# Decay and rate of an RWKV-7 layer: two small matmuls, once per block of 448 tokens instead of once per step of 128

## The chip, the cores and the metric

The kernel runs on one core of a Trainium2 chip. The metric is the device time of one execution in microseconds. Times given are from the hardware profiler and from repeated timed runs. The engines: TensorE (PE, with its weight loads PEld), VectorE (DVE), ScalarE (ACT), GpSimd (POOL) and SyncE (SP), which here issues almost all DMAs, in its program order.

## The reference

One inference step of one hybrid decoder layer, with 2048 prompt tokens and 64 sample tokens (8 requests of 8). The width is 1024. One input projection gives everything: `z = h @ w_in`. Its first 1792 columns are mixed with those of the token before (`zs = z + (z_prev - z) * mu`) and feed an RWKV-7 mixer of 8 heads of 64; the others feed a pooling mixer and two gates. Then follow an output projection and a feed-forward part of 4096. The lines that the change is about:

```python
r = zs[..., :512]; k = zs[..., 512:1024]; v = zs[..., 1024:1536]
lw = zs[..., 1536:1600]          # 64 columns
la = zs[..., 1600:1664]          # 64 columns
w_log = -softplus(-(decay0 + tanh(lw) @ w_decay2)) - 0.5      # w_decay2: 64 x 512
decay = exp(-exp(w_log))
a_in  = sigmoid(a0 + la @ w_a2)                                # w_a2: 64 x 512
kk = k * k_k, normalised per head; k = k * (1 + (a_in - 1) * k_a)
s  = s * decay + (s @ -kk) (kk * a_in)^T + v k^T ; y = s @ r   # per token, per head
```

## The kernel before

The 2112 tokens are cut into five blocks. A block is the width of most matmuls: 384, 448, 448, 448 (384 of the prompt and the 64 sample tokens, block 3) and 384 columns. Activations lie with the features on the 128 partitions and the tokens along the row. A large product is made of three fp32r matmuls, high × high, high × low and low × high, since each operand is split into two parts: a high part, rounded to fp32r by a ScalarE cast (L166), and a low part, the rest, from a VectorE subtraction (L167). A unit of weights is 512 KB, loaded by `load_unit` into `raw` (2 buffers) and split into `whi` and `wlo` (3 buffers each); 24 matmuls use a unit.

Stage A of a block (`stage_A`) is the input projection. Ten tiles of 128 columns come first, numbered m = 12, 13, 0 to 7 (`lerp_tile`): a tile has 24 matmuls into one PSUM tile (`pi`) of the ring `mm` of four. VectorE scales it into `zr` (L476), ScalarE and VectorE do the shift (`zs`, L495 and L496), and a DMA stores it to the DRAM tensor `zd` of the block (L506). m = 12 holds `lw` on its first 64 rows and `la` on the other 64. `zr`, `zs` and many more come from the ring `st`, five tiles of 128x512. Behind tile 7 `values` follows: tokens on the rows, four units `wv_0` to `wv_3`, each used for all token tiles in turn; three of its PSUM tiles (`pv`) come from the ring `mm`, and a fourth from the ring `wk` of three. Then come pooling tiles and gates (`gt`).

The recurrence is worked in 17 steps, k0 to k15 of 128 prompt tokens and k16 of the 64 sample tokens (`wkv_sub`). A step first loads what it wants from `zd`: `lw` and `la` (L1040), `zk` and `zr` (L1043), 256 KB each, and the two matrices with their constant rows (L1046, L1047). Then tanh on `lw` (L1050), four fp32 matmuls `psd` of K = 65 (64 rows and a row of ones for the constant), a ScalarE tanh with the factor 0.5 into `td` (L1055), and the same for `psa` and `ta` (L1060); a sigmoid is written as a tanh. VectorE adds one to `td` (L1062), scans and so on; much later in the step come the norm products `pnb` (from `cs` and from `zk`, L1091), the chunk matrices (`p`, `pt`, `pg`) and the state.

All of TensorE's instructions are chained in the order in which the program emits them (`TensorOrder.issue`). That order is woven from a main stream (stages by `ORDER = "A0 A1 A2 M0 A3 F0 M1 A4 F1 M2 F2 M3 F3 M4 F4"`) and the steps: each step is a generator, and a `yield` with a number says how many microseconds of TensorE time are to pass before the next piece. That time is counted by the planner from the costs in `matmul` (`T.now`), not measured. The lists of the other engines are in program order too, as a scheduler places them. In the trace every matmul has the line L150, whatever asks for it.

Of the kernel before, what the change touches and what calls it, by code (L numbers as in the profile page):

```python
# [67 lines left out]
def hybrid_step(ctx: ExitStack, tc: tile.TileContext, a: dict, outs: list):  # L68
# [149 lines left out]
    for b, (g0, n, s) in enumerate(blocks):  # L218
# [4 lines left out]
        yd.append(dr.tile([n + s, DA], F32, name=f"yd{b}"))  # L223
        xd.append(dr.tile([DM, n + s], F32, name=f"xd{b}"))
    wbd = dr.tile([DP, DM], F32, name="wbd")
    vsd = dr.tile([NS, LS + 1, DA], F32, name="vsd")

    def segs(g, n):
# [172 lines left out]
    consts.close()  # L401
    g2c = kp.tile([P, 8], F32, name="g2c")
    G.dma_start(out=g2c, in_=a["norm2_g"].rearrange("(k p) -> p k", p=P))
    consts.close()
    ready = set()
    done = {"p": 0, "s": False, "pooling": False}
# [78 lines left out]
    def lerp_tile(b, hs, m):  # L485
        g0, n, s = blocks[b]
        nt = n + s
        ci = smap[m]
        raw = st(f"zr{b}_{m}")
        zs = st(f"zs{b}_{m}")  # L490
        V.tensor_copy(raw[:, 0:1], carry[:, ci:ci + 1])

        def evac(sz, ps):
            scaled_out(b, raw[:, 1:1 + sz], ps)
            S.activation(zs[:, :sz], raw[:, 1:1 + sz], AF.Copy, scale=omu[:, m:m + 1])  # L495
            V.scalar_tensor_tensor(zs[:, :n], raw[:, 0:n], mu[:, m:m + 1], zs[:, :n], op0=ALU.mult, op1=ALU.add)  # L496
            V.tensor_copy(carry[:, ci:ci + 1], raw[:, n:n + 1])
            if s:
                zp = sp.tile([P, NS, LS], F32, tag="zp", name=f"zp{b}_{m}", bufs=1)
                rv = raw[:, 1 + n:1 + nt].rearrange("p (s t) -> p s t", t=LS)  # L500
                V.tensor_copy(zp[:, :, 1:], rv[:, :, :LS - 1])
                V.tensor_copy(zp[:, :, 0:1], sst[:, ci].unsqueeze(2))
                V.scalar_tensor_tensor(zs[:, n:nt], zp.rearrange("p s t -> p (s t)"), mu[:, m:m + 1], zs[:, n:nt],
                                       op0=ALU.mult, op1=ALU.add)
                V.tensor_copy(shs[:, ci].unsqueeze(2), rv[:, :, LS - 1:LS])
            D.dma_start(out=zd[b][ci * P:(ci + 1) * P, :], in_=zs[:, :nt])  # L506

        yield from col_tile(b, hs, m, evac)

    def values(b, hs):  # L510
        g0, n, s = blocks[b]
# [164 lines left out]
    def stage_A(b):  # L676
        hs = hs_of.pop(b)
        done["pooling"] = True
        if b:
            dgs[b] = diagonals(r1_of[b], tok_tiles(b), f"r1d{b}")  # L680
        for i, m in enumerate((12, 13, 0, 1, 2, 3, 4, 5, 6, 7)):
            if i > 2:
                tick()
            yield from lerp_tile(b, hs, m)
        yield from values(b, hs)
        ready.add(b)
        us = None
        for i, m in enumerate(range(18, 34)):
            done["pooling"] = i < 9
            tick()  # L690
            if i % 2 == 0 and i <= 8:
                if us is not None:
                    pool_state(i // 2 - 1, us)
                if i < 8:
                    us = yield from pool_tile(b, hs, i // 2)
                    tick()
            yield from gate_tile(b, hs, m)
        yield from flush()
# [309 lines left out]
    def t5(nm):  # L1008
        return kw.tile([P, NPAIR, P], F32, tag="t5", name=nm, bufs=8)
# [13 lines left out]
    def wkv_sub(t0, nch, idx, sample):  # L1023
# [9 lines left out]

        zr = t5v("zr")
        zk = t5v("zk")
        lwa = kw.tile([65, 2, P], F32, tag="lw", name=nm + "lw")[:, :, :TT]
        lw, la = lwa[:, 0], lwa[:, 1]
        pieces = [(SB, blocks[SB][1], TT, 0)] if sample else segs(t0, TT)
        for ib, lo, ln, off in pieces:
            D.dma_start(out=lwa[0:64, :, off:off + ln], in_=zd[ib][1024:1152, lo:lo + ln].rearrange("(a p) t -> p a t", a=2))  # L1040
        for dst, r0 in ((zk, 512), (zr, 0)):
            for ib, lo, ln, off in pieces:
                D.dma_start(out=dst[:, :, off:off + ln], in_=zd[ib][r0:r0 + 512, lo:lo + ln].rearrange("(q p) t -> p q t", p=P))  # L1043
        wdec, wa2 = [t5(nm + x).rearrange("p q t -> p (q t)") for x in ("wd", "wa")]
        for w, mat, row in ((wdec, "w_decay2", "decay0"), (wa2, "w_a2", "a0")):
            D.dma_start(out=w[0:64], in_=a[mat])  # L1046
            D.dma_start(out=w[64:65], in_=a[row].unsqueeze(0))  # L1047
        yield LAT[8]
        G.memset(lwa[64:65], 1.0)
        S.activation(lw[0:64], lw[0:64], AF.Tanh)  # L1050
        psd = wk_ps(nm + "psd").rearrange("p (q t) -> p q t", q=4)[:, :, :TT]
        for q in range(4):
            T.matmul(psd[:, q], wdec[0:65, q * P:(q + 1) * P], lw, start=True, stop=True)
        td = t5v("td")
        S.activation(td, psd, AF.Tanh, scale=0.5)  # L1055
        psa = wk_ps(nm + "psa").rearrange("p (q t) -> p q t", q=4)[:, :, :TT]
        for q in range(4):
            T.matmul(psa[:, q], wa2[0:65, q * P:(q + 1) * P], la, start=True, stop=True)
        ta = t5v("ta")
        S.activation(ta, psa, AF.Tanh, scale=0.5)  # L1060
        yield 1.0
        V.tensor_scalar(td, td, 1.0, None, op0=ALU.add)  # L1062
        cs = t5v("cs")
        for q in range(4):
# [464 lines left out]
```

## Time and profile before

| | us |
|---|---|
| median of three timed runs | 3146.9 (3145.25 to 3147.65) |
| the profiled execution | 3151.2 |
| its span on the core | 3149.5 |
| TensorE busy | 3069.2 (97%) |
| VectorE busy | 2068.7 (66%) |
| ScalarE busy | 1254.4 (40%) |
| mean granted clock of TensorE | 0.992 |

"Busy" is the time in which at least one instruction of the engine ran. Matmuls are pipelined: the time that one occupies is the distance between the starts of two, not its own length. Idle time before an instruction is put down to the one that released it, from semaphore events.

### The profile page before, as it was taken

The numbers are of one execution on the slowest core, as the hardware profiler recorded it, in microseconds if no ns is written. First come the engines' busy times: TensorE is split into PE (matmuls) and PEld (weight loads), VectorE is DVE, ScalarE is ACT, GpSimd is POOL, SyncE is SP. The second block draws the span as 40 slices with busy tenths as digits, with TensorE's granted clock in tenths as the row PEclk, the third lists the DMA queues.
The fourth block names the chain that finished last, engine by engine and source line by source line (L and its number), as shares of the span: only waits on it lengthen the run. The fifth ranks groups of instructions, "written<-read, shape, count | busy, mean of one in ns | idle before, by whom it ended". The sixth has DMA issues, their size and how long they took to land.

```text
span 3149.5 us, 55173 instructions
## 1 busy us (share of the span) xinstructions
PE 3069.2 (97%) x21869; PEld 2813.8 (89%) x21869; DVE 2068.7 (66%) x4002; ACT 1254.4 (40%) x2102; POOL 157.4 (5%) x357
## 2 busy tenths in 40 slices
PE   7999999899999999999999999999999999999997
PEld 7898888898899898899989899889898899999997
DVE  5757666586757667785866678567668655466554
ACT  5444433363333434543433344333334333344333
POOL 3000000000000000010000000000001000000000
PEclk9999999999999999999999999999999999999999
DMA  7756665565554455655544356334446343364443
GB/s 220 200 161 171 194 178 145 153 170 141 146 145 128 129 145 179 183 163 161 151 125 115 107 166 172 93 100 134 123 119 196 105 129 116 107 211 131 125 127 106
DMA packets 738662, 462.24 MB, mean 147 GB/s; under 512 B 143649, under 2 KB 715467, under 8 KB 738396
## 3 DMA queue, kind: packets, MB, share of 16 engines
q1 hardware_dynamic: 737476, 457.55, 50.8%
q8 instruction: 172, 2.82, 0.4%
q0 software_dynamic: 928, 1.16, 0.2%
q14 instruction: 86, 0.70, 0.1%
HBM read 388.81 MB, written 65.54 MB: 144 GB/s over the span
## 4 chain that ended last, share of the span: by engine, by line
PE 81%; DVE 7%; DMA 6%; ACT 2%; issue 2%; SPq 1%; POOL 1%; DVEq 0%; POOLq 0%; ACTq 0%
PE pf L150 23%; PE p L150 22%; PE pi L150 18%; PE po L150 4%; PE pv L150 3%; PE pab L150 3%; DMA pin<-pd 1%; DMA gm<-gd 0%; PE gT L150 0%; PE k16py L150 0%; DMA out<-xo 0%; DMA zd<-zs 0%; PE k16pr L150 0%; DVE gm L824 0%; DMA gf<-in_final_norm_g 0%
## 5 line engine op out<-in xcount | busy, mean ns | idle before, releaser
L936 DVE TENSOR_TENSOR acc<-p,acc 128x448 f32<-128x448 f32 (+1 forms) x320 | 183.9, 593 | 195.4 <-PE p L150 191.9
L873 DVE SCALAR_TENSOR_TENSOR rl<-pf,rsc 128x448 f32<-128x448 f32 (+1 forms) x160 | 95.0, 595 | 172.4 <-PE pf L150 170.3
L166 ACT CAST w_3h<-w_3r 128x1024 fp32r<-128x1024 f32 x80 | 84.1, 1051 | 266.9 <-PE p L150 136.1
L166 ACT CAST w_2h<-w_2r 128x1024 fp32r<-128x1024 f32 x80 | 84.1, 1051 | 190.8 <-PE pf L150 85.9
L166 ACT CAST w_1h<-w_1r 128x1024 fp32r<-128x1024 f32 x80 | 84.1, 1051 | 189.7 <-PE p L150 75.4
L166 ACT CAST w_0h<-w_0r 128x1024 fp32r<-128x1024 f32 x80 | 84.2, 1052 | 152.4 <-PE pf L150 80.2
L150 PE MATMUL p<-gh,w_1h 128*128 128x448 f32 (+1 forms) x320 | 114.3, 357 | 3.3 <-ACT gs L735 3.3
L167 DVE TENSOR_TENSOR w_2l<-w_2r,w_2h 128x1024 fp32r<-128x1024 f32 x80 | 97.8, 1223 | 27.2 <-ACT w_2h L166 26.8
L167 DVE TENSOR_TENSOR w_1l<-w_1r,w_1h 128x1024 fp32r<-128x1024 f32 x80 | 97.8, 1223 | 27.1 <-ACT w_1h L166 27.0
L150 PE MATMUL p<-gh,w_1l 128*128 128x448 f32 (+1 forms) x320 | 114.8, 359 | 0.0
L150 PE MATMUL p<-gh,w_2h 128*128 128x448 f32 (+1 forms) x320 | 113.8, 356 | 0.5 <-DVE acc L936 0.5
L150 PE MATMUL p<-gh,w_0l 128*128 128x448 f32 (+1 forms) x320 | 114.2, 357 | 0.0
L150 PE MATMUL p<-gl,w_1h 128*128 128x448 f32 (+1 forms) x320 | 114.1, 357 | 0.0
L167 DVE TENSOR_TENSOR w_0l<-w_0r,w_0h 128x1024 fp32r<-128x1024 f32 x80 | 97.8, 1222 | 24.8 <-ACT w_0h L166 24.6
L150 PE MATMUL p<-gh,w_3h 128*128 128x448 f32 (+1 forms) x320 | 113.8, 356 | 0.0
L150 PE MATMUL p<-gh,w_0h 128*128 128x448 f32 (+1 forms) x320 | 113.8, 355 | 0.0
L150 PE MATMUL p<-gl,w_2h 128*128 128x448 f32 (+1 forms) x320 | 113.6, 355 | 0.0
L150 PE MATMUL p<-gh,w_2l 128*128 128x448 f32 (+1 forms) x320 | 113.4, 354 | 0.0
L150 PE MATMUL p<-gh,w_3l 128*128 128x448 f32 (+1 forms) x320 | 113.3, 354 | 0.0
L150 PE MATMUL p<-gl,w_3h 128*128 128x448 f32 (+1 forms) x320 | 113.3, 354 | 0.0
L150 PE MATMUL p<-gl,w_0h 128*128 128x448 f32 (+1 forms) x320 | 107.1, 355 | 3.7 <-DVE gl L878 3.7
L167 DVE TENSOR_TENSOR w_3l<-w_3r,w_3h 128x1024 fp32r<-128x1024 f32 x80 | 97.5, 1219 | 17.5 <-ACT w_3h L166 17.3
(3862 smaller groups left out, 9793.9 us busy)
## 6 DMA issues: line engine op xcount, KB each, us to landing
w_0r<-in_w_ff SPq DMA_DIRECT2D x80, 512.0 KB
w_1r<-in_w_ff SPq DMA_DIRECT2D x80, 512.0 KB
w_2r<-in_w_ff SPq DMA_DIRECT2D x80, 512.0 KB
w_3r<-in_w_ff SPq DMA_DIRECT2D x80, 512.0 KB
gd<-gt SPq DMA_DIRECT2D x48, 224.0 KB
gm<-gd SPq DMA_DIRECT2D x48, 224.0 KB
gf<-in_final_norm_g SPq DMA_DIRECT2D x36, 256.0 KB
out<-xo SPq DMA_DIRECT2D x15, 512.0 KB
```

The lines of the kernel that those rows point to most:

```text
L150: self.issue(nc.tensor.matmul(out, lhsT, rhs, start=start, stop=stop), cost)
L166: S.copy(hi[:, :used], raw[:, :used])
L167: V.tensor_tensor(lo[:, :used], raw[:, :used], hi[:, :used], op=ALU.subtract)
L873: V.scalar_tensor_tensor(rl[:, :nt], ps[:, :nt], 0.0, rs, op0=ALU.max, op1=ALU.mult)
L936: V.tensor_tensor(acc[:, m, :nt], pss[m][:, :nt], acc[:, m, :nt], op=ALU.add)
```

## The change

The second products of decay and rate leave the steps. In stage A, ahead of tile m = 6 (i == 8), `lora_load` loads the 128 rows of `lw` and `la` back from `zd`: each set of 64 rows twice, on rows 0 to 63 and on rows 64 to 127 of one `st` tile. It loads `w_decay2` and `w_a2` twice in the same manner (four loads of 128 KB) and casts them: rows 0 to 63 hold the high part, rows 64 to 127 the low part. Behind tile 7, ahead of `values`, `lora` makes for each of the two matrices and each of its four column groups: one fp32r matmul with 128 rows (high weights and low weights, both with the high activations), one with 64 rows (high weights, low activations), a ScalarE tanh with the bias out of PSUM into an `st` tile, and a DMA of that tile to the new DRAM tensor `tda`. The steps load `td` and `ta` from there, 256 KB each, and lose the products, their weights and the first tanh, and one `yield 1.0`.

```diff
+    tda = [dr.tile([2 * DA, n + s], F32, name=f"tda{b}") for b, (g0, n, s) in enumerate(blocks)]
...
+    lbias = kp.tile([P, 8], F32, name="lbias")
+    for i, nm in enumerate(("decay0", "a0")):
+        G.dma_start(out=lbias[:, 4 * i:4 * i + 4], in_=a[nm].rearrange("(q p) -> p q", p=P))
+    V.tensor_scalar(lbias, lbias, 0.5, None, op0=ALU.mult)
...
+    def lora_load(b):
+        nt = blocks[b][1] + blocks[b][2]
+        xs = [st(f"lx{b}_{i}")[:, :nt] for i in range(2)]
+        raw = wp.tile([P, 1024], F32, tag="raw", name=f"lr{b}r", bufs=2)
+        hi = wp.tile([P, 1024], F32R, tag="whi", name=f"lr{b}h")
+        for i, mat in enumerate(("w_decay2", "w_a2")):
+            for h in range(2):
+                r = slice(h * 64, h * 64 + 64)
+                D.dma_start(out=xs[i][r], in_=zd[b][1024 + 64 * i:1088 + 64 * i, :])
+                D.dma_start(out=raw[r, i * DA:(i + 1) * DA], in_=a[mat])
+        S.copy(hi, raw)
+        V.tensor_tensor(hi[64:128], raw[64:128], hi[64:128], op=ALU.subtract)
+        return xs, hi
+
+    def lora(b, xs, w):
+        nt = blocks[b][1] + blocks[b][2]
+        S.activation(xs[0], xs[0], AF.Tanh)
+        for i in range(2):
+            xh = op_.tile([P, NB], F32R, tag="gh", name=f"lh{b}_{i}", bufs=4)[:, :nt]
+            xl = op_.tile([P, NB], F32R, tag="gl", name=f"ll{b}_{i}", bufs=4)[0:64, :nt]
+            S.copy(xh, xs[i])
+            V.tensor_tensor(xl, xs[i][0:64], xh[0:64], op=ALU.subtract)
+            for q in range(4):
+                c = slice(i * DA + q * P, i * DA + (q + 1) * P)
+                ps = mm_ps(f"lo{b}_{i}_{q}")[:, :nt]
+                T.matmul(ps, w[:, c], xh, start=True, stop=False)
+                yield
+                T.matmul(ps, w[0:64, c], xl, start=False, stop=True)
+                yield
+                td = st(f"td{b}_{i}_{q}")[:, :nt]
+                S.activation(td, ps, AF.Tanh, scale=0.5, bias=lbias[:, 4 * i + q:4 * i + q + 1])
+                D.dma_start(out=tda[b][c, :], in_=td)
...
+            if i == 8:
+                held = lora_load(b)
             yield from lerp_tile(b, hs, m)
+        yield from lora(b, *held)
         yield from values(b, hs)
...
-        for ib, lo, ln, off in pieces:
-            D.dma_start(out=lwa[0:64, :, off:off + ln], in_=zd[ib][1024:1152, lo:lo + ln].rearrange("(a p) t -> p a t", a=2))
+        td, ta = t5v("td"), t5v("ta")
+        for dst, r0 in ((td, 0), (ta, DA)):
+            for ib, lo, ln, off in pieces:
+                D.dma_start(out=dst[:, :, off:off + ln], in_=tda[ib][r0:r0 + DA, lo:lo + ln].rearrange("(q p) t -> p q t", p=P))
...
-        for w, mat, row in ((wdec, "w_decay2", "decay0"), (wa2, "w_a2", "a0")):
-            D.dma_start(out=w[0:64], in_=a[mat])
-            D.dma_start(out=w[64:65], in_=a[row].unsqueeze(0))
         yield LAT[8]
-        G.memset(lwa[64:65], 1.0)
-        S.activation(lw[0:64], lw[0:64], AF.Tanh)
...
-        for q in range(4):
-            T.matmul(psd[:, q], wdec[0:65, q * P:(q + 1) * P], lw, start=True, stop=True)
-        td = t5v("td")
-        S.activation(td, psd, AF.Tanh, scale=0.5)
...
-        for q in range(4):
-            T.matmul(psa[:, q], wa2[0:65, q * P:(q + 1) * P], la, start=True, stop=True)
-        ta = t5v("ta")
-        S.activation(ta, psa, AF.Tanh, scale=0.5)
-        yield 1.0
```

What the change moves is read at three places. The first is ScalarE's list in block 1 around the shift of tile 7 (`zs1_7`); `wv1_1h` to `wv1_3h` are casts of value weights, `vt1_0` the first reading of a value product, `k1nbs` a piece of step 1. Before:

```order
L495 ACTIVATE zs1_6_2734<-zr1_6_2733,omu_289 128x448
L210 COPY n1_2_128c0_2781<-n1_2_128tp0_2776 128x512
L166 CAST wv1_2h_2935<-wv1_2r_2934 128x1024
L212 ACTIVATE h2h4_2294<-n1_2_128c0_2781,g1c_137 128x128 x4
L1098 COPY k1nbs_2835<-k1pnb_2826 16x128
L495 ACTIVATE zs1_7_2793<-zr1_7_2792,omu_289 128x448
L166 CAST wv1_3h_2972<-wv1_3r_2971 128x1024
L166 CAST wi1_14h_3098<-wi1_14r_3097 128x1024
L166 CAST wi1_18h_3136<-wi1_18r_3135 128x1024
L534 ACTIVATE vt1_0_3055<-pv1_0_2848,r1_1_563 128x256
```

After, with `td1_i_q` the added tanh out of the added product `lo1_i_q`:

```order
L1125 COPY k1nbs_2877<-k1pnb_2868 16x128
L166 CAST wv1_1h_3016<-wv1_1r_3015 128x1024
L500 ACTIVATE zs1_7_2847<-zr1_7_2846,omu_294 128x448
L548 ACTIVATE td1_0_0_2919<-lo1_0_0_2916,lbias_441 128x448
L548 ACTIVATE td1_0_1_2925<-lo1_0_1_2922,lbias_441 128x448
L548 ACTIVATE td1_0_2_2932<-lo1_0_2_2928,lbias_441 128x448
L548 ACTIVATE td1_0_3_2938<-lo1_0_3_2935,lbias_441 128x448
L548 ACTIVATE td1_1_0_2949<-lo1_1_0_2945,lbias_441 128x448
L548 ACTIVATE td1_1_1_2955<-lo1_1_1_2952,lbias_441 128x448
L166 CAST wv1_2h_3053<-wv1_2r_3052 128x1024
L548 ACTIVATE td1_1_2_2961<-lo1_1_2_2958,lbias_441 128x448
L548 ACTIVATE td1_1_3_2968<-lo1_1_3_2964,lbias_441 128x448
```

Eight tanhs stand behind the shift of tile 7. The cast of the third value weights, ahead of that shift before, now stands behind six of them.

The second place is SyncE's list at the same stretch. `zd1_111` is the DRAM tensor of `zs`, `tda1_137` the new one; rows that end in `in_w_in` are weight loads, `k1sve` and `k1svo` belong to step 1. Before:

```order
L215 DMA xd2_122<-n1_2_128c0_2781 128x4x128
L164 DMA wv1_3r_2971<-in_w_in 128x2x512
L506 DMA zd1_111<-zs1_6_2734 128x448
L164 DMA wi1_14r_3097<-in_w_in 128x8x128
L1158 DMA k1sve_2960<-k1vt_2927 64x512
L1159 DMA k1svo_2961<-k1vt_2927 64x512
L506 DMA zd1_111<-zs1_7_2793 128x448
L164 DMA wi1_18r_3135<-in_w_in 128x8x128
L164 DMA wi1_19r_3213<-in_w_in 128x8x128
L164 DMA wi1_15r_3265<-in_w_in 128x8x128
```

After:

```order
L164 DMA wv1_2r_3052<-in_w_in 128x2x512
L511 DMA zd1_111<-zs1_6_2790 128x448
L549 DMA tda1_137<-td1_0_0_2919 128x448
L549 DMA tda1_137<-td1_0_1_2925 128x448
L164 DMA wv1_3r_3136<-in_w_in 128x2x512
L511 DMA zd1_111<-zs1_7_2847 128x448
L549 DMA tda1_137<-td1_0_2_2932 128x448
L549 DMA tda1_137<-td1_0_3_2938 128x448
L549 DMA tda1_137<-td1_1_0_2949 128x448
L549 DMA tda1_137<-td1_1_1_2955 128x448
L1185 DMA k1sve_3038<-k1vt_3005 64x512
L1186 DMA k1svo_3039<-k1vt_3005 64x512
```

The stores of the tanhs come in between the stores of tiles 6 and 7 and the weight loads; two of them ahead of the store of tile 7, and six ahead of the load of `wi1_14`.

The third place is SyncE's list where step 5 loads what it wants, during stage A of block 3; `vd3` and `pd3` are stores of that stage. Before:

```order
L164 DMA wi3_20r_8594<-in_w_in 128x8x128
L1043 DMA k5zk_8417<-zd1_111 128x4x128
L1043 DMA k5zr_8416<-zd1_111 128x4x128
L1046 DMA k5wd_8422<-in_w_decay2 64x512
L1047 DMA k5wd_8422<-in_decay0 1x512
L1046 DMA k5wa_8423<-in_w_a2 64x512
L1047 DMA k5wa_8423<-in_a0 1x512
L164 DMA wi3_21r_8631<-in_w_in 128x8x128
```

After:

```order
L164 DMA wi3_14r_8574<-in_w_in 128x8x128
L164 DMA wi3_18r_8639<-in_w_in 128x8x128
L164 DMA wi3_19r_8674<-in_w_in 128x8x128
L1084 DMA k5td_8462<-tda1_137 128x4x128
L1084 DMA k5ta_8463<-tda1_137 128x4x128
L1087 DMA k5zk_8461<-zd1_111 128x4x128
L1087 DMA k5zr_8460<-zd1_111 128x4x128
L164 DMA wi3_15r_8741<-in_w_in 128x8x128
L577 DMA vd3_124<-vt3_256_8550 128x512
```

Four loads stand where six stood, beside the load of `lw` that stood further up. They now come ahead of the weight load of tile 15, and behind that of tile 19.

On TensorE the sixteen matmuls `lo` of a block follow the last matmul of tile 7 directly, and the first value product (`pv`) follows them; the other pieces of the steps stand at slightly other places than before.

## Rows read from the trace of the kernel before

**Rows 1.** The page: head, busy time, granted clock, DMA share in 40 slices

```profile
span 3149.5 us, 55173 instructions
...
PE 3069.2 (97%) x21869; PEld 2813.8 (89%) x21869; DVE 2068.7 (66%) x4002; ACT 1254.4 (40%) x2102; POOL 157.4 (5%) x357
...
PEclk9999999999999999999999999999999999999999
DMA  7756665565554455655544356334446343364443
```

**Rows 2.** The page: chain that ended last, its shares by engine

```profile
PE 81%; DVE 7%; DMA 6%; ACT 2%; issue 2%; SPq 1%; POOL 1%; DVEq 0%; POOLq 0%; ACTq 0%
```

**Rows 3.** TensorE's waits: line <- releaser: us in total, times, longest

```profile
PE k15pnb L150 <- DVE k15zk L1091: 3.6, 1, 3.6
...
PE k13pnb L150 <- DVE k13zk L1091: 1.7, 1, 1.7
```

**Rows 4.** Timeline of TensorE, step 5: start, us, instruction, count

```profile
802.17 1.05 PE L150 MATMUL k5psd<-k5lw,k5wd 65*128 65x128 f32 x8
803.06 1.06 PE L150 MATMUL k5psa<-k5lw,k5wa 65*128 65x128 f32 x8
803.87 0.45 PE L150 MATMUL pi<-h3l,wi_19h 128*128 128x448 f32 x1
```

**Rows 5.** Timeline of TensorE, step 12, with the idle time before

```profile
1774.42 1.13 PE L150 MATMUL k12psd<-k12lw,k12wd 65*128 65x128 f32 x8 [0.90 <-DMA k12wd<-in_w_decay]
```

**Rows 6.** Timeline of TensorE, end of tile 7, blocks 2 and 0

```profile
461.29 0.36 PE L150 MATMUL pi<-h2l,wi_7h 128*128 128x448 f32 x1
461.49 0.39 PE L150 MATMUL pv<-wv_0h,h2h 128*128 128x512 f32 x1
...
73.33 0.33 PE L150 MATMUL pi<-h0l,wi_7h 128*128 128x384 f32 x1
73.50 0.39 PE L150 MATMUL pv<-wv_0h,h0h 128*128 128x512 f32 x1
```

**Rows 7.** Timeline of VectorE and of ScalarE, block 2, tile 7

```profile
462.32 0.62 DVE L476 TENSOR_TENSOR zr<-pi,rs 128x448 f32<-128x448 f32 x1
...
463.03 0.67 ACT L495 ACTIVATE zs<-zr,omu 128x448 f32<-128x448 f32 x1 [0.29 <-DVE zr L476]
```

**Rows 8.** One tile's view (k5psd), its reader: ns min/median/max, start

```profile
L1055 ACT ACTIVATE k5td<-k5psd x1: 597/597/597, 803.3 to 803.3; 128x512 f32<-128x512 f32 x1
```

**Rows 9.** Chain (start, us, what); timelines of SyncE and ScalarE

```profile
58.39 6.53 DMA zd<-zs
...
79.08 4.56 DMA zd<-zs
...
240.19 0.62 SPq L1040 DMA_DIRECT2D k2lw<-zd  x1
...
242.62 0.31 ACT L1050 ACTIVATE k2lw<-k2lw 64x128 f32<-64x128 f32 x1 [1.86 <-DMA k2lw<-zd]
```

**Rows 10.** Block 0: window (busy us, PEclk, DMA share, GB/s); ScalarE

```profile
60.00:80.00 20.00, 20.00 (x110) 18.84 (x109) 13.19 (x32) 11.28 (x24) 1.54 (x1) 1.00 0.81 231
...
64.65 1.05 ACT L166 CAST wi_7h<-wi_7r 128x1024 fp32r<-128x1024 f32 x1 [1.61 <-DMA wi_7r<-in_w_in]
...
77.22 0.62 ACT L495 ACTIVATE zs<-zr,omu 128x384 f32<-128x384 f32 x1
...
91.28 1.04 ACT L166 CAST wi_18h<-wi_18r 128x1024 fp32r<-128x1024 f32 x1 [6.91 <-DMA wi_18r<-in_w_in]
```

**Rows 11.** TensorE after two waits: timelines, then windows with PEclk

```profile
94.03 0.69 PE L150 MATMUL pi<-h0h,wi_14h 128*128 128x384 f32 x1 [3.57 <-DVE vt L532]
...
2126.07 1.05 PE L150 MATMUL k13pnb<-k13zk,selw 128*16 128x128 f32 x8 [1.68 <-DVE k13zk L1091]
...
94.00:97.00 3.00, 2.96 (x9) 2.97 (x10) 1.60 (x2) 3.00 (x9) 0.00 (x0) 0.50 0.64 173
2126.00:2130.00 4.00, 3.93 (x28) 3.16 (x28) 3.93 (x8) 1.01 (x2) 0.00 (x0) 1.00 0.49 135
```

More of the change, by code (lines that the diff above doesn't have):

```diff
@@ L1035, in wkv_sub @@
         zk = t5v("zk")
-        lwa = kw.tile([65, 2, P], F32, tag="lw", name=nm + "lw")[:, :, :TT]
-        lw, la = lwa[:, 0], lwa[:, 1]
         pieces = [(SB, blocks[SB][1], TT, 0)] if sample else segs(t0, TT)
-        for ib, lo, ln, off in pieces:
-            D.dma_start(out=lwa[0:64, :, off:off + ln], in_=zd[ib][1024:1152, lo:lo + ln].rearrange("(a p) t -> p a t", a=2))
+        td, ta = t5v("td"), t5v("ta")
+        for dst, r0 in ((td, 0), (ta, DA)):
+            for ib, lo, ln, off in pieces:
+                D.dma_start(out=dst[:, :, off:off + ln], in_=tda[ib][r0:r0 + DA, lo:lo + ln].rearrange("(q p) t -> p q t", p=P))
         for dst, r0 in ((zk, 512), (zr, 0)):
@@ L1043, in wkv_sub @@
                 D.dma_start(out=dst[:, :, off:off + ln], in_=zd[ib][r0:r0 + 512, lo:lo + ln].rearrange("(q p) t -> p q t", p=P))
-        wdec, wa2 = [t5(nm + x).rearrange("p q t -> p (q t)") for x in ("wd", "wa")]
-        for w, mat, row in ((wdec, "w_decay2", "decay0"), (wa2, "w_a2", "a0")):
-            D.dma_start(out=w[0:64], in_=a[mat])
-            D.dma_start(out=w[64:65], in_=a[row].unsqueeze(0))
         yield LAT[8]
-        G.memset(lwa[64:65], 1.0)
-        S.activation(lw[0:64], lw[0:64], AF.Tanh)
-        psd = wk_ps(nm + "psd").rearrange("p (q t) -> p q t", q=4)[:, :, :TT]
-        for q in range(4):
-            T.matmul(psd[:, q], wdec[0:65, q * P:(q + 1) * P], lw, start=True, stop=True)
-        td = t5v("td")
-        S.activation(td, psd, AF.Tanh, scale=0.5)
-        psa = wk_ps(nm + "psa").rearrange("p (q t) -> p q t", q=4)[:, :, :TT]
-        for q in range(4):
-            T.matmul(psa[:, q], wa2[0:65, q * P:(q + 1) * P], la, start=True, stop=True)
-        ta = t5v("ta")
-        S.activation(ta, psa, AF.Tanh, scale=0.5)
-        yield 1.0
         V.tensor_scalar(td, td, 1.0, None, op0=ALU.add)
```

## The prediction

> **What bounds the kernel now.** I read the head of the page first, then the chain, then what TensorE waited for, then single stretches. The head shows TensorE busy for 3069.2 us of the 3149.5 us span, at the upper level of its clock in nearly every slice, ScalarE for 40% [rows 1]. The chain that ended last runs through TensorE for 81% of the span [rows 2]. So the first question on an edit is how many TensorE microseconds it takes away, the second whether it makes TensorE wait. Waits are few today; the largest inside a step are those of the norm product (`pnb`) for VectorE's `zk`, 3.6 and 1.7 us [rows 3]. The sum below is made against the profiled run of 3151.2 us (1.7 us of it outside the span). The three timed runs have a median of 3146.9 us, 4.3 us lower, and I carry that difference over.
>
> **Removed from TensorE.** In step 5 the two products occupy TensorE from 802.17 to the next matmul at 803.87, 1.70 us [rows 4]. The sample step costs as much by the same reading, so 17 steps make 28.9 us. Steps 6, 12, 13 and 15 hold 2.1 us more, idle or stretched, of which 0.90 us is step 12's wait for its weight load [rows 5]; no such load remains. Together −31.0 us, all on the engine that bounds. What goes beside it (a tanh on 64 rows, two tanhs on ScalarE, a memset on GpSimd) lay under TensorE's work: nothing.
>
> **Added to TensorE.** Sixteen matmuls per block, each over the block's columns. At 448 columns one starts 0.20 us after another, at 384 columns 0.17 us [rows 6]. Three blocks have 448 and two 384: 3 × 16 × 0.20 + 2 × 16 × 0.17 = 15.0 us. Without any wait the change is worth −16.0 us, and that is the budget for waits: 3.2 us a block.
>
> **What the added matmuls wait for.** They stand in TensorE's order between the last tile of the shifted part and the value product, and fill eight PSUM tiles from a ring of four. Each is emptied by one ScalarE tanh into a tile of the five-deep `st` ring, from which a store leaves. The copies and subtractions that feed them stand far ahead of T and lie beside tiles 6 and 7: nothing. I follow block 2, with T the end of its tile 7, 461.49 [rows 6].
> - ScalarE takes its instructions in order, and the first added tanh stands behind the shift of tile 7. That begins at 463.03 and lasts 0.67 us, since VectorE's scaling of the tile starts only at 462.32 [rows 7]. So the first tanh starts at T + 2.2.
> - One emptying of 128x512 from PSUM took 0.60 us [rows 8]; I take that. The tanhs end at T + 2.8, 3.4, 4.0 and 4.6, while TensorE fills four tiles by T + 1.6 and then needs the first one back. The eighth tile is filled at T + 5.0 rather than T + 3.2.
> - The first value product takes the slot of the fifth tile. With ScalarE as the only limit it is free at T + 5.2: a stall of 2.0 us.
> - The fifth tanh, though, writes into the `st` tile of the first, whose store must have landed. The trace has no such store on a quiet queue with a user at once. The nearest rows are a 64 KB load, 2.4 us from issue (240.19) to its user (242.62), and two 192 KB stores of block 0 on the chain, 6.53 and 4.56 us [rows 9]. From 2.4 to 6.5 I take 3.5: above the load, because 224 KB are more and weight loads share the queue; below the two stores, because block 0 is where DMA is busiest. The fifth tanh then ends at T + 2.9 + 3.5 + 0.6 = T + 7.0, and the stall is 3.75 us against T + 3.25. The ends give 2.0 (landing hidden by ScalarE) and 6.75.
>
> Blocks 1 to 4 at 3.75 each make 15.0 us (8.0 to 27.0). Behind the waiting tanh ScalarE has the cast of the third value weights, which TensorE wants two units (2 × 24 × 0.20 = 9.6 us) later: covered. SP has behind the stores that wait the loads of later weights, priced below.
>
> The Trainium skill, "DMA: Bandwidth & Descriptors", section "Anatomy of one DMA", gives, for transfers that GpSimd issues, about 2.0 us fixed each, mostly until the write is confirmed, plus the bytes at 436 GB/s. By that a 224 KB store is an estimated 2.5 us and the sum some 4 us lower. The two stores of block 0 took longer than the page's figure.
>
> **Block 0.** DMA is 0.81 busy at 60 to 80 us, and ScalarE waits for weights there (1.61 us before 64.65, 6.91 us before 91.28) [rows 10]. T is 73.50 [rows 6], but the shift of tile 7 begins at 77.22 and lasts 0.62 [rows 10], so the first tanh starts at T + 4.3. With the store's 4.56 us the fifth ends at about T + 10.1 instead of T + 2.8: 7.3 us. Without the landing it ends at T + 4.3 + 5 × 0.6 = T + 7.3, a stall of 4.5. The upper end is 16: the slower store (9.3), and all of ScalarE's 6.91 us for late weights passed on to TensorE.
>
> **The clock.** After 3.57 us idle at 94.03, the nine matmuls of the next 3 us ran at 0.50 granted, the 1.2 GHz level; after 1.68 us idle at 2126.07 the clock stayed at 1.00, the 2.4 GHz level [rows 11]. Nine matmuls of 384 columns are 9 × 0.17 = 1.5 us at the upper level, so one fall costs 1.5 us. A stall of 3.75 us in the value product is like the first of these rows, but parts of it lie apart. I count the fall for block 0 and two others: 4.5 us (0 to 7.5).
>
> **Weights.** The added weights hold one of three `whi` tiles from tile 6 on, so the casts of tile 7 and of the first value weights start one unit (4.8 us) later. TensorE waited for no cast there before; its own work of that unit is the cover. If it is gone, one late load is worth ScalarE's 1.61 us [rows 10], in five blocks 8: from 0 to 8 I take 1.5, block 0 alone.
>
> **Steps.** A step's loads grow from 836 KB in seven DMAs (64 + 2 × 256 + 2 × 130) to 1024 KB in four. SP has less to issue; the last load lands later. Step 12 is the one place where a late load reached TensorE, by 0.90 us [rows 5]: 0 to 4, I take 1. In return the way to `zk` loses a wait on TensorE and two tanhs; of the 5.3 us in [rows 3] I take 2 back (from all 5.3 back to 3 more, should late loads lengthen that wait).
>
> **Sum.** −31.0 + 15.0 + 15.0 + 7.3 + 4.5 + 1.5 + 1 − 2 = +11.3. On 3151.2 that is 3162.5, less 4.3 it is 3158 us.
>
> **The rivals.**
> A, faster: the ring keeps up. Stores land before the fifth tanh wants its tile, ScalarE alone limits, the clock does not fall, the weights come in time, and the norm products gain all of 5.3: −16.0 + 8.0 + 4.5 − 5.3 = −8.8, 3138 us. For it: ScalarE is idle more than half the time, and TensorE waits for no store today. Against it: 2.0 us a block come from ScalarE's order alone. It decides where the waits together stay under 16.0 − 6.3 = 9.7 us.
>
> The Trainium skill, "Perfetto Trace Analysis", section "Matmuls", says that groups which rotate through PSUM banks let one group's emptying overlap the next one's matmuls. By that alone A would hold at its best, with no stall at all. The trace shows it for tiles of 24 matmuls.
>
> Against that overlap stands the size of a group here: two matmuls, 0.40 us, against 0.60 to empty one [rows 6, 8], with four banks and a late start.
>
> B, no difference: stalls of 2.75 us in blocks 1 to 4 and 5 in block 0, no fall of the clock, saving and waits cancel: −16.0 + 11 + 5 = 0, 3147 us. It needs landings near the quiet load's 2.4 us.
>
> C, much slower: block 0 costs 16, landings are near 4.6 us in the others (5 us of stall each), the clock falls in all and the weights cost 4: −16.0 + 20 + 16 + 7.5 + 4 = +31.5, 3178 us. Against it: after block 0 DMA is busy little over half of the time [rows 1].
>
> D, the saving does not come: a step's pieces are placed by TensorE's planned time, which the change shortens by 1.7 us and one pause of a step; if each of the 17 steps then waits 1 us more at its later pieces, the sum rises by 17, to 3175. The pieces stand next to nearly the same tiles as before, so I give it little.
>
> **How the numbers follow.** This kernel can be told from no change beyond about 0.2%, 6.3 us: faster is under 3140.6, slower over 3153.2. My case has 0.47 (own range 3153 to 3168), C 0.09, D 0.04, B 0.25, A 0.15; the first three are slower. The size of the stalls is rough, and the range leaves out half of C and two thirds of A: 3141 to 3177.
>
> **What would show it.** TensorE's busy time falls by some 16 us less the falls of the clock. Its list of waits gets rows at the added products with ScalarE as the releaser (0.3 to 1.3 us each) and one of 2 to 4 us at a value product, in every block, longest in block 0, and the fifth tanh waits for the first one's store. If the value product starts within 0.5 us of the last added matmul, the ring argument is wrong and A is right. If the granted clock is 1.00 behind these stalls, the clock term is wrong. If the new idle time sits in the steps, it is D.

## The result and the profile after

The changed kernel takes 3222.4 us (median of four runs, 3212.0 to 3226.6) against 3147.3 (3145.3 to 3148.6) for the kernel before: a ratio of 1.0234 [1.0220, 1.0248], 75 us slower. The forecast was 3158 us with a range of 3141 to 3177. The sign was right; the size was not, and most of the reasons were not either. The profiled execution took 3226.6 us. The page's head of the kernel after, to be read against [rows 1]:

```profile
span 3224.9 us, 54842 instructions
...
PE 3106.2 (96%) x21677; PEld 2818.7 (87%) x21677; DVE 2083.3 (65%) x4018; ACT 1266.1 (39%) x2111; POOL 152.6 (5%) x342
...
PEclk8999999989999999999999999999999999999999
```

The span grew by 75.4 us. TensorE's busy time grew by 37.0 (3069.2 to 3106.2) though it has 192 matmul records fewer, and its time that is not busy grew by 38.4 (80.3 to 118.7, span less busy). The mean granted clock fell from 0.992 to 0.979. That share of the two spans is 0.008 × 3149.5 = 25 and 0.021 × 3224.9 = 68 us, so the clock alone is some 40 us. The chain, against [rows 2]:

```profile
PE 75%; DVE 11%; DMA 8%; issue 2%; ACT 2%; SPq 1%; POOL 0%; DVEq 0%; POOLq 0%; ACTq 0%
```

TensorE lost 6 points of it, VectorE gained 4 and DMA 2. TensorE's waits of the kernel after (line, releaser: us in total, times, longest), against [rows 3]:

```profile
PE p L150 <- DVE gl L922: 17.7, 9, 3.7
...
PE pab L150 <- DVE gm L868: 7.6, 5, 3.1
...
PE pi L150 <- DVE r L180: 3.3, 1, 3.3
PE pi L150 <- ACT wi_6h L166: 3.3, 1, 3.3
...
PE lo L150 <- ACT td L548: 1.6, 2, 1.1
```

The rows of `p` and `pab` with the same releasers in the kernel before:

```profile
PE p L150 <- DVE gl L878: 3.7, 1, 3.7
...
PE pab L150 <- DVE gm L824: 1.1, 1, 1.1
```

The new waits are not where the forecast put them. The added products (`lo`) wait for ScalarE's tanh for 1.6 us in the whole kernel, where some 22 us of stalls had been forecast there and at the value products. The large feed-forward products (`p`, `pab`), which the change doesn't touch, wait for VectorE.

For the comparisons (the other kernels are explained in the next section) I worked four numbers out of each trace: TensorE's idle time (the sum of all its waits), the clock's cost (the time that its matmuls took longer than at the upper level, 2.4 GHz), the time that the added products occupy (from start to start, waits left out), and the same for `psd` and `psa`. The part of the clock's cost that falls inside the added products is in both columns. The last column tells TensorE's order: in kernels with the same letter the traces have TensorE's matmuls in the same order, row for row, with those left out that only one of them has (added products, removed products, gates); a few records are missing in each trace.

| kernel | ratio to before [95%] | span | idle | clock | added | psd, psa | order |
|---|---|---|---|---|---|---|---|
| before | 1 | 3149.5 | 62.7 | 23.1 | 0 | 29.3 | a |
| after | 1.0234 [1.0220, 1.0248] | 3224.9 | 101.2 | 60.8 | 34.9 | 0 | d |
| before_noyield | 1.0061 [1.0046, 1.0076] | 3168.4 | 78.7 | 26.9 | 0 | 29.1 | b |
| rem_only | 1.0059 [1.0042, 1.0076] | 3170.7 | 94.5 | 44.1 | 0 | 0 | b |
| rem_gate | 0.9999 [0.9989, 1.0008] | 3146.0 | 78.1 | 30.7 | 0 | gates 2.4 | a |
| add_only | 1.0243 [1.0228, 1.0259] | 3226.4 | 86.0 | 51.5 | 41.7 | 29.0 | c |
| after_k128 | 1.0205 [1.0188, 1.0221] | 3208.1 | 107.1 | 47.3 | 22.5 | 0 | d |
| add_spread | 1.0197 [1.0181, 1.0212] | 3209.7 | 90.5 | 38.8 | 16.8 | 29.0 | nearly c |
| after_gate | 1.0164 [1.0147, 1.0181] | 3202.9 | 84.9 | 52.1 | 40.2 | gates 2.4 | c |
| spread_late | 1.0079 [1.0064, 1.0094] | 3174.7 | 84.9 | 41.1 | 18.3 | 0 | its own |

### The profile page after: what moved, and what is told of

It is laid out like the page before. It is cut to its first block, busy times and chain, and to the rows that moved or that the text cites. A ratio compares the mean times of both kernels' runs of the same rounds, so it can differ in the third digit from the quotient of the medians.

```text
span 3224.9 us, 54842 instructions
## 1 busy us (share of the span) xinstructions
PE 3106.2 (96%) x21677; PEld 2818.7 (87%) x21677; DVE 2083.3 (65%) x4018; ACT 1266.1 (39%) x2111; POOL 152.6 (5%) x342
## 4 chain that ended last, share of the span: by engine, by line
PE 75%; DVE 11%; DMA 8%; issue 2%; ACT 2%; SPq 1%; POOL 0%; DVEq 0%; POOLq 0%; ACTq 0%
PE p L150 20%; PE pf L150 19%; PE pi L150 15%; PE po L150 5%; PE pv L150 3%; PE pab L150 2%; DMA gm<-gd 1%; PE lo L150 1%; DMA out<-xo 1%; PE gT L150 0%; DMA pin<-pd 0%; DMA zd<-zs 0%; DVE acc L980 0%; PE k16py L150 0%; PE k16pr L150 0%
```

## The experiments

**The two halves apart.** In the quoted expectations R and L are two theories of the result: R, that a step's load of `vq`, issued with that of `vt`, waits for a free tile of the ring `t5`, and VectorE then waits for both; L, that the removed pause lets the steps' pieces come too early. The first kernel has the removal alone: `td` and `ta` are loaded from rows of `zd`, so decay and rate are not computed in it. The second has the addition alone: the steps are as before, and nobody reads `tda`.

```diff
 # rem_only
-            if i == 8:
-                held = lora_load(b)
...
-        yield from lora(b, *held)
...
-                D.dma_start(out=dst[...], in_=tda[ib][r0:r0 + DA, lo:lo + ln]...)
+                D.dma_start(out=dst[...], in_=zd[ib][r0:r0 + DA, lo:lo + ln]...)
 # add_only: the steps of the kernel before, stage A of the kernel after
```

> Removal alone: the steps load td and ta, 256 KB each, from rows 0 to 1023 of zd, which are there anyway; nothing is computed for them in stage A (so decay and rate are other numbers than the reference's). Theory R (the ring of step tiles): in the changed kernel the tile vq of every step got the slot of the same step's kkn, so its load is issued only when kkn has been read for the last time, some 14 us later than before, SyncE stands still at it and VectorE waits for the load. Then the removal alone is slower than the kernel before in spite of 31 us less on TensorE: 3165 to 3195 us. Theory S (all of the loss sits in stage A, at the added matmuls and what they hold up): 3147 - 31 = about 3116 us.

> Addition alone: stage A computes and stores the new tensor, nobody reads it, the steps are as in the kernel before. Theory R: the added matmuls take the 37.5 us that the trace of the changed kernel shows from their first one to the value product in five blocks, and little else is lost: 3180 to 3195 us. Theory S: the whole loss is here: 3222 + 31 = about 3253 us.

The removal alone took 3171.5 us, +0.59%, where it takes 29 us of matmuls away. The addition alone took 3228.3, +2.43%. So both halves cost, and neither is what the forecast had: the removal was priced at −31 and came out near +19, the addition at some +43 (15 of matmuls, 22 of stalls, the rest clock and weights) and came out near +77. They do not add up: together they cost 75, not 96, and TensorE's order is another one in each of the three (b, c and d in the table). TensorE's waits in the removal alone have those of the feed-forward products again:

```profile
PE p L150 <- DVE gl L919: 19.8, 6, 4.4
...
PE pab L150 <- DVE gm L865: 6.5, 5, 2.0
```

**A ring or the pause.** Nine tiles instead of eight in the steps' ring `t5` (paid for by adding `lng` in place of `lnb`, whose tile is left out), and the lost pause given back:

```diff
 # after_b9
-    lnb = kp.tile([P, NPAIR, HD], F32, name="lnb")
+    lnb = lng
...
-        return kw.tile([P, NPAIR, P], F32, tag="t5", name=nm, bufs=8)
+        return kw.tile([P, NPAIR, P], F32, tag="t5", name=nm, bufs=9)
 # after_late; rem_late is the same edit on rem_only
-        yield LAT[8]
+        yield LAT[8] + 1.5
+        yield 1.0
```

> The changed kernel with nine tiles in the ring of step tiles instead of eight (to make room one constant is dropped and the scale lng is added in place of the shift lnb, the same instruction on another tile). vq then takes the slot of td, which is free after the scans. Theory R: the load of vq is issued some 10 us earlier in a step, VectorE's 36.5 us of waits for vt go, and 35 to 65 us come back: 3155 to 3190 us. Theory L (a step's VectorE work starts too early against its loads) and theory S: no change beyond 10 us: 3212 to 3230 us.

> The changed kernel with the pause between a step's loads and its first VectorE instruction restored to what it was before in planned TensorE time (5.75 + 1.5 + 1.0, times 1.15, instead of 5.75 times 1.15); vq still has the slot of kkn. Theory L: VectorE's 11.8 us of waits for td go, and with them the crowding of VectorE at the gl subtractions: 3165 to 3195 us. Theory R: the wait for vq stays: 3205 to 3230 us.

With nine tiles nothing changed (3224.6 us), nor did the waits for `vt`: R falls. With the pause 3208.0, +1.78% [1.63, 1.93]: some 14 us came back, less than a fifth.

**Controls, and rows of the added products.** Two edits of the kernel before that change no work, to see what a mere shift costs: the planner's clock moved on at the place of the added matmuls, and the pause taken out. And in the kernel after, the second matmul of each pair on all 128 rows (for rows 64 to 127 the low activations multiply the low weights as well), alone and with the pause:

```diff
 # before_shift (before_shift2: 32 in place of 16)
+        T.now += 16 * ((blocks[b][1] + blocks[b][2]) / 2400.0 + 0.0135)
 # before_noyield
-        yield 1.0
 # after_k128, late_k128
-            V.tensor_tensor(xl, xs[i][0:64], xh[0:64], op=ALU.subtract)
+            V.tensor_tensor(xl, xs[i], xh, op=ALU.subtract)
-                T.matmul(ps, w[0:64, c], xl, start=False, stop=True)
+                T.matmul(ps, w[:, c], xl, start=False, stop=True)
```

> The kernel before, with one line: at the place of the added matmuls the planner's clock is advanced by what they are planned to take (3.2 us in a block of 448, 2.8 in one of 384). No instruction is added or taken away; the steps only fall at other places between the large products. Theory P (places: the kernel before stands at places that suit it, and any shift makes VectorE's and ScalarE's work of the steps collide with what the large products wait for): 15 to 50 us slower, 15 to 30 us more idle time on TensorE and some 5 to 10 more falls of its clock at 2 to 3 us each. Theory W (the loss beside the added matmuls comes from the added work itself, its weights, stores and tiles): within 6 us of the kernel before.

> The kernel before without the pause yield 1.0 between a step's tanh of psa and its first VectorE instruction, as in the change; nothing else. Theory P: 10 to 45 us slower, by more idle time and more falls of the clock. Theory W: within 6 us.

> The changed kernel, with the second matmul of each pair on all 128 rows instead of 64 (the low activations on both halves, which adds the product of low weights and low activations); TensorE's order is the same. Theory K (a matmul on 64 rows behind one on 128 rows, and the other way round, starts 0.39 us after it instead of 0.20): the added matmuls then start 0.20 us apart at 448 columns, and the 35 us that they take fall by 13 to 18 us unless ScalarE's emptying takes over as the limit (then the value product waits): 3200 to 3212 us. If the 0.39 us have another reason (the PSUM tile, the weights): no change, 3220 to 3230 us.

> Both: the restored pause and the second matmul on 128 rows. If the two gains of 15 us each add up: 3190 to 3200 us. If the emptying or the places take the second one back: 3200 to 3212 us.

The controls cost +0.17% [0.07, 0.27] and +0.61% [0.46, 0.76] (3154.0 and 3169.0 us). A pause of 1 us taken from each step, with all products left in, costs as much as the whole removal, and TensorE's order is then that of the removal alone (b), row for row. So the removal's 19 us go with this order, and at the same order the 29 us of matmuls less gain nothing: 1.0059 without them, 1.0061 with them. TensorE's waits at the feed-forward products come with the pause too, though smaller:

```profile
PE p L150 <- DVE gl L878: 9.1, 3, 5.4
...
PE pab L150 <- DVE gm L824: 5.7, 3, 3.5
```

The 128-row version took 3214.9 us, with the pause 3201.8 (+1.68% [1.51, 1.85]); TensorE's order was the same row for row in the first. In the kernel after, TensorE's timeline at the end of tile 7 of block 1 (start, us, instruction, rows*columns):

```profile
269.46 0.36 PE L150 MATMUL pi<-h1h,wi_7l 128*128 128x448 f32 x1
269.66 0.37 PE L150 MATMUL pi<-h1l,wi_7h 128*128 128x448 f32 x1
...
270.29 0.47 PE L150 MATMUL lo<-lh,lr1h 128*128 128x448 f32 x1
270.68 0.46 PE L150 MATMUL lo<-ll,lr1h 64*128 64x448 f32 x1
271.08 0.47 PE L150 MATMUL lo<-lh,lr1h 128*128 128x448 f32 x1
271.47 0.47 PE L150 MATMUL lo<-ll,lr1h 64*128 64x448 f32 x1
```

With 128 rows in both, same place:

```profile
268.73 0.36 PE L150 MATMUL lo<-ll,lr1h 128*128 128x448 f32 x1
268.93 0.36 PE L150 MATMUL lo<-lh,lr1h 128*128 128x448 f32 x1
269.12 0.37 PE L150 MATMUL lo<-ll,lr1h 128*128 128x448 f32 x1
269.33 0.36 PE L150 MATMUL lo<-lh,lr1h 128*128 128x448 f32 x1
```

Matmuls of tile 7 start 0.20 us apart. The added ones, whose rows alternate between 128 and 64, start 0.39 to 0.40 apart, and 0.19 to 0.21 apart where both have 128 rows. Twice the arithmetic in the second matmul took half the time; the granted clock in the kernel after was still 0.97 in this stretch (below). The edit took 12.4 us of occupancy away (34.9 to 22.5), and the stretch that follows also got its clock back. Windows of the kernel after (stretch; length, busy time of PE, PEld, DVE, ACT, POOL; PEclk, DMA share, GB/s):

```profile
270.00:276.90 6.90, 6.90 (x25) 3.23 (x24) 4.43 (x10) 4.97 (x8) 0.00 (x0) 0.97 0.87 238
276.90:285.00 8.10, 8.10 (x30) 6.25 (x30) 1.92 (x2) 3.20 (x4) 0.00 (x0) 0.82 0.89 307
```

And of the 128-row version:

```profile
268.40:273.10 4.70, 4.21 (x20) 2.61 (x17) 3.63 (x9) 4.21 (x7) 0.00 (x0) 1.00 0.74 244
273.10:281.20 8.10, 7.29 (x32) 5.36 (x32) 1.64 (x2) 3.89 (x5) 0.00 (x0) 1.00 0.93 309
```

In the kernel after TensorE had no idle time at all from 270.0 to 285.0, and yet the value products right behind the added ones ran at a mean of 0.82: the lower level for part of the stretch, the upper one for the rest. With the 128-row pair they ran at 1.00. Of the 26 us (12.4 occupancy, 13.5 clock, partly the same time) 16.8 came back in the profiled executions and 7.5 in the medians. 5.9 us went to more idle time, since now the ring binds: TensorE's waits in the 128-row version have

```profile
PE p L150 <- DVE gl L922: 16.8, 8, 3.7
...
PE lo L150 <- ACT td L548: 7.1, 8, 2.1
```

and 2.2 us more at value products. In the kernel after, with pairs of 0.79 us, there were 1.6 us of these waits; that the slow pairs gave ScalarE the time is argued from that.

**Both halves mended.** The removal alone with the pause; the addition alone spread out (loads ahead of the third tile, casts ahead of the fourth, 128 rows, one pair after each tile from the fourth on, two after the last); the change with that; and that with the pause:

```diff
 # add_spread; spread is the same in the kernel after; spread_late adds the pause
-            if i == 8:
+            if i == 2:
                 held = lora_load(b)
+            if i == 3:
+                held = lora_split(b, *held)
             yield from lerp_tile(b, hs, m)
-        yield from lora(b, *held)
+            for g in ((), (i - 3,), (6, 7))[(i > 2) + (i > 8)]:
+                yield from lora(b, *held, g)
```

> Removal alone (td and ta loaded from rows of zd, nothing computed for them) with the pause between a step's loads and its first VectorE instruction restored. Theory L (the removal alone lost 50 us of its 31 us saving because a step's VectorE work comes some 8 us earlier and meets the large products' work): most of that comes back, 3120 to 3145 us, faster than before. Theory R (tiles of the ring, the load of vq late) or the greater loads as the cause: 3155 to 3175 us.

> Addition alone, in another place: weights and activations are split at the second tile of stage A into tiles of the gh and gl rings (no weight tile is held), both matmuls on 128 rows, and one pair follows each of the tiles m = 1 to 7 (two pairs the last) instead of all eight in a row; nobody reads the result. Theory E (the loss at the added products comes from eight short groups in a row: emptying, st tiles, the whi tile, the rows changing between 128 and 64): the addition costs the matmuls' 16 us and up to 15 more: 3165 to 3185 us instead of 3228. If the loss is in the stores, the loads or the work on ScalarE and VectorE as such: 3200 to 3230 us.

> The changed kernel with the addition spread in the same way; the steps as in the change. Theory E and L together: the steps' part is that of the removal alone (+19 us), the addition 16 to 31: 3185 to 3200 us.

> The same with the restored pause. E and L together: 3150 - 31 + 16 and 5 to 25 for waits left: 3140 to 3165 us; if either is wrong 3175 to 3210 us.

The removal with the pause took 3163.6 us (+0.52% [0.37, 0.67]), still over the kernel before, in a TensorE order of its own: L explains at most a small part. The spread addition alone took 3211.2, the change with it 3213.1 (+2.06% [1.89, 2.23]), that with the pause 3174.8, the fastest full version, +0.79%. In the last, TensorE still waits for what was to be hidden; 12.8 us of it are one wait in block 0, at 58.33, where the loads of `lw` and `la` are issued at 53.74. Without it the time would still be over that of before (an estimate: 3174.8 − 12.8 = 3162):

```profile
PE lo L150 <- ACT lh L540: 16.7, 2, 12.8
```

**The gate.** What else the removal changes is seen at step 8 (SP: issue of a DMA; DVE: instructions of VectorE). Before:

```profile
1209.94 0.43 SPq L1043 DMA_DIRECT2D k8zk<-zd  x1
...
1224.07 0.42 DVE L1062 TENSOR_SCALAR k8td<-k8td 128x512 f32<-128x512 f32 x1
1224.40 0.68 DVE L1336 TENSOR_TENSOR k7yc<-k7yc,k7vt 128x512 f32<-128x512 f32 x1
...
1226.44 0.62 SPq L1146 DMA_DIRECT2D k8vt<-vd  x1
...
1234.42 0.68 DVE L1151 TENSOR_TENSOR k8vq<-k8vq,k8vt 128x512 f32<-128x512 f32 x1
```

After:

```profile
1237.41 0.58 SPq L1084 DMA_DIRECT2D k8td<-tda  x1
...
1241.85 0.43 DVE L1089 TENSOR_SCALAR k8td<-k8td 128x512 f32<-128x512 f32 x1 [1.04 <-DMA k8td<-tda]
...
1263.67 0.68 DVE L1363 TENSOR_TENSOR k7yc<-k7yc,k7vt 128x512 f32<-128x512 f32 x1
...
1266.19 0.61 SPq L1173 DMA_DIRECT2D k8vt<-vd  x1
...
1270.73 0.69 DVE L1178 TENSOR_TENSOR k8vq<-k8vq,k8vt 128x512 f32<-128x512 f32 x1 [5.90 <-DMA k8vt<-vd]
```

Before, the first VectorE instruction of step 8 stands 14.1 us behind the loads, because `td` comes out of products that wait for their turn in TensorE's list, and the tail of step 7 is all but done: its last reading of `k7vt` is the next instruction. After, it stands 4.4 us behind them. From there on VectorE's list weaves the chain of step 8 into the tail of step 7, whose last reading comes 21.8 us later. The load of `k8vt` is issued only behind that reading, 28.8 us after the first of the loads shown instead of 16.5, and VectorE waits 5.90 us for it, with everything that stands behind. So the removed products had a second office: they were a gate. To test it, the removal alone got a gate back: a one-column matmul in TensorE's list, whose result (−0.5) goes into the constant of `td` + 1. The edit also gives the planner back the products' time (`T.now += 1.7`) and the pause:

```diff
 # rem_gate; after_gate is the same in the kernel after
-        V.tensor_scalar(td, td, 1.0, None, op0=ALU.add)
+        gate = wk_ps(nm + "gate")[:, 0:1]
+        T.matmul(gate, ident, mhalf, start=True, stop=True)
+        gs = kw.tile([P, 1], F32, tag="gs", name=nm + "gs", bufs=2)
+        S.copy(gs, gate)
+        T.now += 1.7
+        yield 1.0
+        V.tensor_scalar(td, td, gs, 0.5, op0=ALU.subtract, op1=ALU.add)
 # spread_gate: spread with the gate, pairs one tile later, block 0 from its seventh tile on
```

> Removal alone (td and ta loaded from rows of zd) with a gate: at the place of the removed products one fp32 matmul of one column, whose result (-0.5) VectorE's first instruction of the step subtracts before it adds 0.5; the planner's clock and the pause are as before. Theory G: a step's VectorE work falls back to about 11 us behind its loads, the waits for vt go, idle time on TensorE falls from 95 to 60-75 us: 3120 to 3140 us, faster than the kernel before. If loads or tiles are the cause: 3155 to 3175 us, as without a gate.

> The changed kernel with the same gate and nothing else. Theory G: the removal's 50 us come back, 3170 to 3190 us; otherwise 3205 to 3225 us.

> The addition spread over the tiles of stage A (pairs on 128 rows, one tile later than in the run before, in block 0 from its fourth lerp tile from the end on) with the gate. Theory G and E: 3150 - 31 + 16 + 2 for the gates and 0 to 20 for waits: 3135 to 3160 us.

> The kernel before with the planner's clock advanced in each block by twice the added matmuls' planned time (6.4 us, 5.6 in blocks of 384), no instruction added or removed. If shifts as such cost some 20 us (theory P), 3160 to 3180 us; if before_shift (+5 us) is typical, 3145 to 3160 us.

> The kernel before with all pauses of the steps 4% longer (factor 1.20 instead of 1.15), no instruction added or removed. Theory P: 3160 to 3190 us; otherwise 3145 to 3160 us.

The removal with the gate took 3151.0 us, no different from before (0.9999 [0.9989, 1.0008]), 20 us less than without; the change with it 3203.6, 19 us less. Step 8 of the removal with the gate:

```profile
1212.75 0.43 SPq L1081 DMA_DIRECT2D k8td<-zd  x1
...
1226.28 0.48 DVE L1092 TENSOR_SCALAR k8td<-k8td,k8gs 128x512 f32<-128x512 f32 x1
...
1229.03 0.67 DVE L1366 TENSOR_TENSOR k7yc<-k7yc,k7vt 128x512 f32<-128x512 f32 x1
...
1231.03 0.61 SPq L1176 DMA_DIRECT2D k8vt<-vd  x1
...
1239.51 0.68 DVE L1181 TENSOR_TENSOR k8vq<-k8vq,k8vt 128x512 f32<-128x512 f32 x1
```

The delays are those of before again (13.5 and 18.3 us), and there is no wait. Over steps 1 to 15 the first VectorE instruction stands a median of 11.1 us behind the loads before, 4.5 in the removal alone, 5.1 with the pause and 10.3 with the gate; VectorE's waits for `vt` are 0, 28.5, 36.7 and 0 us. So it is shown that the removed products set the pace of the steps, and that a gate can stand in for them.

What this pace is worth in time is not shown. The gate's edit also puts TensorE's order back to that of the kernel before (a), row for row, and the same change of order with all products in place (`before_noyield` against before) is worth the same 20 us. In that pair VectorE has no wait for `vt` in either kernel. After and `after_gate` have different orders too (d and c), and no two kernels with the same order differ by the gate alone.

What the removal saved is still not gained, though order and pace are those of before. TensorE's waits with the gate:

```profile
PE p L150 <- DVE gl L919: 5.5, 4, 3.8
PE gT L150 <- DVE lin L766: 5.2, 1, 5.2
PE k15pnb L150 <- DVE k15zk L1121: 4.8, 1, 4.8
PE k3pnb L150 <- DVE k3zk L1121: 4.7, 1, 4.7
```

The norm products now wait for `zk` in seven steps for 17.2 us, against 5.3 before [rows 3]. All idle time grew by 15.4 us, 14.9 of them ahead of matmuls of the steps; the clock costs 7.6 us more, the gates 2.4. That is 25 of the 29 us that were saved, and more than half of the 25 are waits in the steps: in this order the products' time had been cover for VectorE's work there. In the addition's order (c) it was so less, if at all: there the change with the gate is 25 us faster than the addition alone (1.0164 against 1.0243), so most of the 29 us were gained. Why one order gives them and the other does not stays open.

The spread change with the gate took 3185.4 (+1.05% [0.90, 1.20]). The two last controls took 3164.6 (+0.49% [0.34, 0.64], a shift of twice the size) and 3151.8 (+0.10% [0.01, 0.20], the planner's factor `STRETCH` at 1.20 in place of 1.15). No version is faster than the kernel before. The gate and the pause together were not tried.

## Why the prediction was wrong, step by step

- *"Together −31.0 us, all on the engine that bounds. What goes beside it … lay under TensorE's work: nothing."* This is the step that failed first. The 29 us left TensorE's list, as said; but the removal alone made the kernel 19 us slower, so this step is off by 50 us. Two things stood at nothing in it. The products' time was cover: with the order and the pace of before (`rem_gate`) 25 of the 29 us came back as waits of TensorE in the steps, lower clock and gates, and the time was 0.9999 of before. And the lost pause gives TensorE another order, which costs 19 us with all products left in (`before_noyield`). A row that could have warned stood in the trace: `td` + 1 of step 8 comes 14 us behind the load of `zk`, where the nearest load with a user at once took 2.4 [rows 9]; so something other than data sets its time.
- *"In return the way to `zk` loses a wait on TensorE and two tanhs"*: this small term held (the norm products' waits for `zk` fell from 5.3 to 1.7 us), but the same removal let the steps start early on VectorE, with 37.8 us of VectorE's waits for `vt`. Rival D named the planned time and the lost pause as the cause and 17 us as the price, and got 0.04; the lost pause alone cost 19 (`before_noyield`). D looked for the new waits in the steps; in the removal alone the waits of the steps' matmuls grew by 3 us and those at `p`, `pab` and `po` by 26.
- *"At 448 columns one starts 0.20 us after another"*: the row read was of matmuls with 128 rows throughout [rows 6]. The alternating pairs took 0.39 to 0.40, more where the clock was down: 34.9 us instead of 15.0. The 128-row version shows that the 64 rows of the second matmul do it; whether it is the alternation or 64 rows as such was not tried.
- *The stalls, 15.0 + 7.3*: 1.6 us of waits for the tanhs. The value product starts 0.59 to 0.67 us behind the start of the last added matmul in all five blocks, without idle time in between, so the stall forecast there is absent and the ring argument fell. Matmuls and stalls together had been 37.3 us; the occupancy from the first added matmul to the value product, waits in it, sums to 41.4 in the five blocks. The size came out near by accident. With pairs at 0.20 the stalls appear, but only 7.1 and 2.2 us.
- The Trainium skill, "Perfetto Trace Analysis", section "Matmuls", on groups that rotate through PSUM banks, would have had no stall at all. The kernel after comes close to it (1.6 us); the 128-row version, with 7.1 us in eight waits, shows where two-matmul groups outrun the emptying.
- *The clock, 4.5 us*: some 38 (60.8 against 23.1). It had been tied to idle time, three falls of 1.5 us. The kernel after has 21 stretches below the upper level against 9 before, 2.9 us each on average, and some without idle time in front, as at 276.4 us.
- *Weights, 1.5 us*: in four blocks TensorE waits for the casts or subtractions of tile 6's weights, up to 3.3 us twice. The row of the waits above that names `r` is one of them: the matmul behind it, at 256.30, takes `wi_6l`, whose subtraction ran at 255.02 behind pieces of step 1 on VectorE.
- *Step 12's wait, 0.90 us* [rows 5] is gone, as said.

**What stays open.** The addition alone has some 20 us more idle time and lower clock in feed-forward and output stages, in which nothing is edited; its largest waits:

```profile
PE p L150 <- DVE gl L922: 15.5, 4, 5.6
...
PE pab L150 <- ACT xo L1003: 5.9, 2, 5.0
```

That is of the size that a mere shift of the pieces costs (+5, +19, +15 and +3 us in the four controls), but that it is such a shift is argued, not shown: no run has the addition's order (c) without the added products. Nor is it shown why the halves together cost 20 us less than their sum; as each has its own order, they need not add up.

## What to carry to other kernels

Before work is taken off the engine that bounds, ask what it covers: at two orders of TensorE (a, b) 29 us less of it gained nothing here, since that engine then waited more and ran longer at the lower clock, and at a third (c) most of it was gained. Look also at what its place in an ordered list holds back: a reader that runs much later than its loads land is paced by something else, and a one-column gate can stand in for it. Price an added matmul by a row of its own shape and its own neighbours, not by its columns alone. In a kernel whose lists are planned by hand, run a neutral shift first: here four of them cost 3 to 19 us, as much as a change of 0.6%. Compare kernels whose order is the same, or the order's price is taken for that of the edit.

## What the runs showed of the hardware

- Matmuls whose row counts alternate between 128 and 64 started 0.39 to 0.40 us apart at 448 columns, and 0.19 to 0.21 where both had 128 rows and nothing waited, with the same order on the engine. Over 80 matmuls the occupancy went from 34.9 to 22.5 us.
- The granted clock fell to 0.82 in a stretch (276.9 to 285.0) in which TensorE had been busy without a gap since 270.0; behind the same products with 128 rows in each it stayed at 1.00. In the kernel after the clock went to its lower level (1.2 GHz) in or right behind the alternating matmuls in all five blocks, and in three of them (at 276.4, 812.3 and 1450.6 us) TensorE had had no wait since the products began.
